# The high parts of the attentions' weights: copied by ScalarE, or brought rounded by transfers that GpSimd begins

## The chip, the cores and the metric

The kernel runs on one core of one Trainium2 chip, as one program. The metric is the device time of an execution in microseconds (us). The times before are three runs; beside them one execution was taken with the hardware profiler.

## What is computed

Three transformer layers on 256 positions of width 1024, in float32: two layers of a first kind, then one of a second kind.

```python
def hybrid_layer(x, ...):            # twice
    proj = x @ w_in
    a_in, b_in, c_in = jnp.split(proj, [A_COLS, A_COLS + B_COLS], axis=-1)
    o_a = dilated_mixture(...)        # 6 heads
    o_b = diff_attention(...)         # 4 heads
    o_c = causal_attention(...)       # 6 heads, low-rank q and kv
    h = layer_norm(DEEPNORM_ALPHA * x + heads @ w_o, ln1_g, ln1_b)
    ffn = (jax.nn.silu(h @ w_gate) * (h @ w_up)) @ w_down
    return layer_norm(DEEPNORM_ALPHA * h + ffn, ln2_g, ln2_b)

def second_block(x, c, ...):         # once
    h = _rms_norm(x, g_pre_mix[l]) * (1.0 + sc_m) + sh_m
    y = _hybrid_mixer(h, ...)         # 8 heads of sparse attention in three branches, 8 heads of indexed attention
    x = x + ga_m * _rms_norm(y, g_post_mix[l])
    h = _rms_norm(x, g_pre_ffn[l]) * (1.0 + sc_f) + sh_f
    x = x + ga_f * _rms_norm(_swiglu(h, w_gate_up[l], w_down[l]), g_post_ffn[l])
```

## The kernel before

**Three products for one.** Every large product of an activation with a weight is made of three matmuls in the type fp32r (`mm3`, lines 274 to 278). Both operands are split into a high part, the value rounded to fp32r, and a low part, the rest: high by high (L276), high by low, low by high. A low part needs its high part first. In the trace `xh`, `xl` are the parts of an activation, `hi`, `lo` those of a weight.

**Pieces of weights.** All weights come as a list of pieces, `plan`, in the order of use; a piece is 128 partitions by at most 2048 columns, 1 MB. Class `Weights` walks it. `_load` begins a piece's transfer on SP's queue into one of three `raw` buffers (L105). `_half` splits half a piece: ScalarE copies `raw` to `hi`, which rounds (L129), and VectorE subtracts `hi` from `raw` into `lo` (L130). The pools `hi` and `lo` have six half-piece buffers each, so three pieces. `get` hands out the next piece; it keeps loads three pieces ahead and splits one piece ahead. Pieces of kind "raw" are used unsplit.

**Order of the pieces.** For each of the two layers: `w_inc` (2 pieces) and `w_inbv` (in layer 1 `w_inbv` first), `w_u` raw, `w_inbqk` (2), `w_inav` (2), `w_inaqk` (3), `w_o` (4), then the feed-forward: `w_gate` and `w_up` (11 each) with `w_down` pieces among them, the last three of layer 0 and the last two of layer 1 at the end. For the second block: `w2_kc`, `w2_vc`, `w2_nq` (2 each), `w2_mi`, `w2_iq` (2), `w2_uk` raw, `w2_dq` (2), `w2_out` (4), then its feed-forward.

**Order of the work.** The program is written in order; the framework's planner gives each engine its own order from its own costs, and every engine then works its queue strictly in that order. Blocks with a raised priority are drawn forward: scores and values of the attentions, and the norms at the end of a sublayer (`ending`, L393). Matmuls of the projections fill TensorE while an attention waits for its softmax: for each pair of heads VectorE adds the bias and takes the minimum (L315), ScalarE takes the exponentials (`e`, L316), the probabilities are scaled (L550 or L552), transposed on TensorE (`pt`, L271), copied by ScalarE (`ptsb`, L586) and multiplied with the values (`ob`, L559).

**Hand-overs.** At the end of a feed-forward the last `w_down` pieces are held together while TensorE finishes rows 0 to 127 and then rows 128 to 255. The norm of the first half runs beside the matmuls of the second. Then `fill` (L861) runs the next layer's first projections on the first half, while the norm of the second half runs: `w_inbv` and `w_inc` for layer 1, `w2_kc` (`kp.run(0)`) for the second block, which later runs `kp.run(1)`, `vp.run(0)` and so on (L1129). The norms take their inverse root on GpSimd (`rsqrt`, L306 to L312), an addition and a power. GpSimd has hardly any other work.

Of the kernel before, what the change touches and what calls it, by code (L numbers as in the profile page):

```python
# [11 lines left out]
F32R = mybir.dt.float32r  # L12
AF = mybir.ActivationFunctionType
# [11 lines left out]
WARM = 11  # L25
PUTB = 2
NHI = 6
ROWS = 16
STEPS = ('00', '0001', '0001001', '0001001', '0001001')

# [61 lines left out]
class Weights:  # L92


    def __init__(self, tc, pools, plan, ahead, split_ahead):
        self.nc, self.pools, self.plan = tc.nc, pools, plan
        self.ahead, self.split_ahead = ahead, split_ahead
        self.loaded, self.split, self.at = 0, 0, 0
        self.raws, self.parts, self.out = {}, {}, {}

    def _load(self):
        i = self.loaded
# [6 lines left out]
    def start(self, pieces):  # L109
# [10 lines left out]
            self.out[i] = self._getter(i)  # L120
        self.loaded = self.split = 2

    def _half(self, i, h):
        _, _, nk, w = self.plan[i]
        t, n = self.raws[i], nk * w // 2
        hi = self.pools["hi"].tile([128, 1024], F32R, tag="hi", name="hi")
        lo = self.pools["lo"].tile([128, 1024], F32R, tag="lo", name="lo")
        c = slice(h * n, h * n + n)
        self.nc.scalar.activation(hi[:, :n], t[:, c], AF.Copy)  # L129
        self.nc.vector.tensor_tensor(lo[:, :n], t[:, c], hi[:, :n].bitcast(F32), op=OP.subtract)  # L130
        self.parts.setdefault(i, []).append((hi, lo))

# [12 lines left out]
    def _split(self):  # L145
        i = self.split
        _, kind, nk, w = self.plan[i]
        while self.loaded <= i:
            self._load()
        if kind == "split":  # L150
            for h in range(2):
                self._half(i, h)
            self.out[i] = self._getter(i)
        else:
            self.out[i] = self.raws.pop(i)
        self.split += 1

    def get(self):
        i = self.at
        self.at += 1  # L160
        n = len(self.plan)
        while self.split <= i:
            self._split()
        while self.loaded < min(n, i + 1 + self.ahead):
            self._load()
        while self.split < min(n, i + 1 + self.split_ahead) and self.plan[self.split][1] == "split":
            self._split()
        return self.out.pop(i)


@with_exitstack
def body(ctx: ExitStack, tc: tile.TileContext, io, out):
# [3 lines left out]
    def pool(name, bufs=1, **kw):  # L176
        return ctx.enter_context(tc.tile_pool(name=name, bufs=bufs, **kw))
# [4 lines left out]
    raw_p = pool("raw", 3)  # L182
    hi_p = pool("hi", NHI)
    lo_p = pool("lo", NHI)
    ln_p = pool("ln", 3)
# [22 lines left out]
    def add(name, *idx, kind="split", nk, w):  # L208
        ap = io[name]
        for i in idx:  # L210
            ap = ap[i]
        plan.append((ap, kind, nk, w))


    def add_ffn(names, idx, held):
        g, u, d = names
        for j in range(NCH):
            add(g, *idx, j, nk=8, w=256)
            add(u, *idx, j, nk=8, w=256)
            if 1 <= j <= held:  # L220
                add(d, *idx, j - 1, nk=2, w=1024)
        for j in range(held, NCH):
            add(d, *idx, j, nk=2, w=1024)

    for l in range(2):
        if l == 1:
            add("w_inbv", l, nk=8, w=256)
        for i in range(2):
            add("w_inc", l, i, nk=4, w=416)
        if l == 0:  # L230
            add("w_inbv", l, nk=8, w=256)
        add("w_u", l, kind="raw", nk=1, w=1920)
        for i in range(2):
            add("w_inbqk", l, i, nk=8, w=256)
        for i in range(2):
            add("w_inav", l, i, nk=4, w=384)
        for i in range(3):
            add("w_inaqk", l, i, nk=8, w=256)
        for i in range(4):
            add("w_o", l, i, nk=2, w=1024)  # L240
        add_ffn(("w_gate", "w_up", "w_down"), (l,), HELD[l])
    for i in range(2):
        add("w2_kc", i, nk=4, w=384)
    for i in range(2):
        add("w2_vc", i, nk=4, w=384)
    for i in range(2):
        add("w2_nq", i, nk=4, w=512)
    add("w2_mi", 0, nk=8, w=240)
    for i in range(2):
        add("w2_iq", i, nk=4, w=512)  # L250
    add("w2_uk", kind="raw", nk=1, w=896)
    for i in range(2):
        add("w2_dq", i, nk=4, w=512)
    for i in range(4):
        add("w2_out", i, nk=2, w=1024)
    add_ffn(("w2_gate", "w2_up", "w2_down"), (), HELD[2])


# [80 lines left out]
    def load_bias(oh):  # L339
# [3 lines left out]
        V.tensor_copy(bsb, pb[:10, :384])  # L343
        bd = dram.tile([ROWS, 10, 384], F32, name="bd")
        nc.scalar.dma_start(bd.rearrange("q h c -> h q c"), bsb[:, None, :].to_broadcast([10, ROWS, 384]))
        for r in range(128 // ROWS):
            p = slice(ROWS * r, ROWS * r + ROWS)
            nc.scalar.dma_start(bias[p], bass.AP(tensor=bd.tensor, offset=bd.offset + 127 - ROWS * r,
                                                 ap=[[3839, ROWS], [384, 10], [1, 256]]))

# [1019 lines left out]
```

## Time and profile before

| | |
|---|---|
| median of three runs | 979.72 us (978.67 to 981.13) |
| the profiled execution | 977.63 us, of which the span from first to last instruction 975.8 |
| TensorE matmuls, weight loads | busy 944.4 us (97%), 834.9 us (86%) |
| VectorE, ScalarE, GpSimd | busy 650.5, 533.2, 29.2 us |
| ScalarE's weight copies, L129 | 284, 293.7 us busy |
| VectorE's subtractions, L130 | 284, 339.1 us busy |
| moved by transfers | 190.55 MB |

Layer 0's attentions last until some 115 us, its feed-forward until some 320, layer 1's until some 430 and 640, the second block's attentions until some 770. In the rows, "out<-in" names the tiles written and read, "x" a count, and "<-" what ended an engine's wait. A matmul's time is its way through the array; the next begins long before it ends, so TensorE can be busy and still have gaps between starts.

### The profile page before, as it was taken

What the parts mean: (1) busy time and instruction counts of PE and PEld (TensorE: products, weight loads), DVE (VectorE), ACT (ScalarE), POOL (GpSimd) and SP (SyncE); (2) the same over time, 40 slices, a digit from 0 to 9 for tenths busy, and PEclk for the clock granted to TensorE, in tenths of its full rate; (3) what the DMA queues carried; (4) which work ended last, traced back from release to release, by engine and by line L of the source; (5) the groups of instructions that cost most, each with busy time, mean ns of one, the idle gap of its engine ahead of it and who ended that gap; (6) DMA issues with size and microseconds to landing.
All of it is one profiled execution on the core that took longest, in us unless ns stands there. A gap on an engine that the chain in (4) does not pass through costs nothing. (4 is left out here: it accounts for less than half of the span.)

```text
span 975.8 us, 16344 instructions
## 1 busy us (share of the span) xinstructions
PE 944.4 (97%) x6378; PEld 834.9 (86%) x6378; DVE 650.5 (67%) x1367; ACT 533.2 (55%) x1023; POOL 29.2 (3%) x54
## 2 busy tenths in 40 slices
PE   8999999999999999999999999889999899999997
PEld 6888689999998888878999999788666699999996
DVE  4648687767678757767767464787688665454543
ACT  4658665444444677655444444555599744344542
POOL 0000000000000100000000000101000100000000
PEclk9999999999999999999999999999999999999999
DMA  8745548877875533447875565365312156555441
GB/s 313 288 100 215 196 176 301 300 278 270 300 254 175 192 131 127 149 179 278 308 277 211 177 242 190 109 242 206 130 45 87 65 173 215 175 181 205 153 153 44
DMA packets 33456, 190.55 MB, mean 195 GB/s; under 512 B 3696, under 2 KB 5346, under 8 KB 15842
## 3 DMA queue, kind: packets, MB, share of 16 engines
q1 hardware_dynamic: 31224, 183.75, 52.9%
q10 hardware_dynamic: 2154, 5.75, 2.0%
q8 instruction: 50, 0.82, 0.3%
q14 instruction: 28, 0.23, 0.1%
HBM read 188.17 MB, written 1.32 MB: 194 GB/s over the span
## 5 line engine op out<-in xcount | busy, mean ns | idle before, releaser
L130 DVE TENSOR_TENSOR lo<-raw,hi 128x1024 fp32r<-128x1024 f32 (+3 forms) x284 | 339.1, 1202 | 99.7 <-ACT hi L129 95.6
L129 ACT ACTIVATE hi<-raw 128x1024 fp32r<-128x1024 f32 (+3 forms) x284 | 293.7, 1041 | 103.1 <-PE acc L278 52.3
L278 PE MATMUL sc<-xh,lo 128*128 128x256 f32 x960 | 271.8, 283 | 0.0
L276 PE MATMUL sc<-xh,hi 128*128 128x256 f32 x960 | 271.7, 283 | 0.0
L277 PE MATMUL sc<-xl,hi 128*128 128x256 f32 x960 | 271.7, 283 | 0.0
L276 PEld LDWEIGHTS sc<-xh,hi 128*128 128x128 f32 x960 | 184.2, 192 | 1.1
L277 PEld LDWEIGHTS sc<-xl,hi 128*128 128x128 f32 x960 | 184.2, 192 | 1.0
L278 PEld LDWEIGHTS sc<-xh,lo 128*128 128x128 f32 x960 | 184.2, 192 | 0.0
L276 PE MATMUL acc<-hi,xh 128*128 128x512 f32 (+4 forms) x384 | 135.2, 354 | 0.4 <-ACT hi L129 0.3
L277 PE MATMUL acc<-lo,xh 128*128 128x512 f32 (+4 forms) x384 | 134.0, 349 | 0.7 <-DVE lo L130 0.6
L278 PE MATMUL acc<-hi,xl 128*128 128x512 f32 (+4 forms) x384 | 133.6, 349 | 0.7 <-DVE xl L298 0.7
L276 PE MATMUL acc<-hi,hh 128*128 128x512 f32 x264 | 103.2, 391 | 0.0
L277 PE MATMUL acc<-lo,hh 128*128 128x512 f32 x264 | 103.2, 391 | 0.0
L278 PE MATMUL acc<-hi,hl 128*128 128x512 f32 x264 | 102.8, 389 | 0.0
L453 ACT ACTIVATE sg<-sc 128x256 f32<-128x256 f32 x60 | 22.6, 376 | 137.9 <-PE sc L278 137.9
L455 DVE TENSOR_TENSOR hm<-sc,sg 128x256 f32<-128x256 f32 x60 | 25.3, 421 | 88.0 <-ACT sg L453 88.0
L276 PEld LDWEIGHTS acc<-hi,xh 128*128 128x128 f32 x384 | 74.4, 194 | 8.5 <-issue 1.5
L277 PEld LDWEIGHTS acc<-lo,xh 128*128 128x128 f32 x384 | 74.4, 194 | 6.7 <-DVE lo L130 1.6
L278 PEld LDWEIGHTS acc<-hi,xl 128*128 128x128 f32 x384 | 74.2, 194 | 6.9 <-DVE xl L298 2.0
L316 ACT ACTIVATE e<-e,sm 128x128 f32<-128x128 f32 (+1 forms) x128 | 56.8, 446 | 12.0 <-DVE sm L315 7.7
L278 PEld LDWEIGHTS acc<-hi,hl 128*128 128x128 f32 x264 | 49.6, 188 | 10.8 <-DVE hl L457 0.2
L276 PEld LDWEIGHTS acc<-hi,hh 128*128 128x128 f32 x264 | 49.7, 188 | 9.8 <-ACT hh L456 0.3
(277 smaller groups left out, 1155.7 us busy)
## 6 DMA issues: line engine op xcount, KB each, us to landing
raw<-in_w_gate SPq DMA_DIRECT2D x33, 1024.0 KB, 4.9
raw<-in_w_up SPq DMA_DIRECT2D x33, 1024.0 KB, 4.9
raw<-in_w_down SPq DMA_DIRECT2D x33, 1024.0 KB, 5.0
ada<-in_w_ada SPq DMA_DIRECT2D x48, 512.0 KB, 5.2
raw<-in_w_o SPq DMA_DIRECT2D x8, 1024.0 KB, 5.2
raw<-in_w_inaqk SPq DMA_DIRECT2D x6, 1024.0 KB, 5.1
raw<-in_w_inbqk SPq DMA_DIRECT2D x4, 1024.0 KB, 6.2
gb<-in_lnrows ACTq DMA_DIRECT2D x4, 1024.0 KB, 6.2
```

What stands on the lines that cost most here:

```text
L129: self.nc.scalar.activation(hi[:, :n], t[:, c], AF.Copy)
L130: self.nc.vector.tensor_tensor(lo[:, :n], t[:, c], hi[:, :n].bitcast(F32), op=OP.subtract)
L276: T.matmul(dst, lh, rh, start=start, stop=False)
L277: T.matmul(dst, lh, rl, start=False, stop=False)
L278: T.matmul(dst, ll, rh, start=False, stop=stop)
L316: A.activation(e, e, AF.Exp, bias=nm, scale=-1.0, accum_out=sm)
L453: A.activation(sg, pg[:, 0, :], AF.Silu)
L455: V.tensor_tensor(hm, pg[:, 1, :], sg, op=OP.mult)
```

## The change

The pieces of layer 0's `w_inav`, `w_inaqk`, `w_o` and all split pieces of the attentions of layer 1 and of the second block get the kind "cast". For these, `_cast` takes two `hi` buffers and begins two transfers on GpSimd's queue, each of half a piece, from DRAM into the fp32r buffer; ScalarE's copy is left out in `_half`, and VectorE subtracts as before from the `raw` buffer, which SP's transfer still fills. `get(i)` begins these transfers for the piece i + 2, one piece before that is split. Layer 0's first pieces and all feed-forward pieces stay as they were, as do the sizes of the pools.

```diff
+SPLIT = ("split", "cast")
...
+    def _cast(self, i):
+        ap, _, nk, w = self.plan[i]
+        n = nk * w // 2
+        his = self.his[i] = []
+        for h in range(2):
+            his.append(self.pools["hi"].tile([128, 1024], F32R, tag="hi", name="hi"))
+            self.nc.gpsimd.dma_start(his[h][:, :n], ap[:, h * n:h * n + n])
...
     def _half(self, i, h):
...
-        hi = self.pools["hi"].tile([128, 1024], F32R, tag="hi", name="hi")
+        cast = i in self.his
+        hi = self.his[i][h] if cast else self.pools["hi"].tile([128, 1024], F32R, tag="hi", name="hi")
...
-        self.nc.scalar.activation(hi[:, :n], t[:, c], AF.Copy)
+        if not cast:
+            self.nc.scalar.activation(hi[:, :n], t[:, c], AF.Copy)
...
-        if kind == "split":
+        if kind in SPLIT:
+            if kind == "cast" and i not in self.his:
+                self._cast(i)
...
-        while self.split < min(n, i + 1 + self.split_ahead) and self.plan[self.split][1] == "split":
+        while self.split < min(n, i + 1 + self.split_ahead) and self.plan[self.split][1] in SPLIT:
             self._split()
+        j = self.split
+        if j < n and j == i + 1 + self.split_ahead and self.plan[j][1] == "cast":
+            self._cast(j)
...
-            add("w_inbv", l, nk=8, w=256)
+            add("w_inbv", l, kind=SPLIT[l], nk=8, w=256)
...
-            add("w_inc", l, i, nk=4, w=416)
+            add("w_inc", l, i, kind=SPLIT[l], nk=4, w=416)
...
-            add("w_inav", l, i, nk=4, w=384)
+            add("w_inav", l, i, kind="cast", nk=4, w=384)
```

`w_inbqk` becomes `SPLIT[l]` in the same way; `w_inaqk`, `w_o` and the second block's `w2_kc`, `w2_vc`, `w2_nq`, `w2_mi`, `w2_iq`, `w2_dq`, `w2_out` become "cast".

## Rows read from the trace of the kernel before

**Rows 1.** The page: TensorE's busy time; GB/s in 40 slices of 24.4 us.

```profile
PE 944.4 (97%) x6378; PEld 834.9 (86%) x6378; DVE 650.5 (67%) x1367; ACT 533.2 (55%) x1023; POOL 29.2 (3%) x54
...
GB/s 313 288 100 215 196 176 301 300 278 270 300 254 175 192 131 127 149 179 278 308 277 211 177 242 190 109 242 206 130 45 87 65 173 215 175 181 205 153 153 44
```

**Rows 2.** Groups by shape: copies and subtraction; busy us, mean ns, idle before.

```profile
L130 DVE TENSOR_TENSOR lo<-raw,hi 128x1024 fp32r<-128x1024 f32 x258 | 313.7, 1224 | 90.8 <-ACT hi L129 86.9 <-PE sc L277 1.4
...
L129 ACT ACTIVATE hi<-raw 128x1024 fp32r<-128x1024 f32 x258 | 271.7, 1058 | 97.8 <-PE acc L278 51.9 <-PE sc L277 33.6 <-PE acc L277 4.7
...
L129 ACT ACTIVATE hi<-raw 128x768 fp32r<-128x768 f32 x16 | 13.2, 840 | 3.5 <-DMA raw<-in_w_inav 1.1 <-PE sc L277 1.0 <-ACT acc L523 0.9
```

**Rows 3.** Stages: length, busy of PE, PEld, DVE, ACT, POOL, clock, DMA.

```profile
28.00:115.00 87.00, 83.94 (x581) 69.94 (x580) 58.07 (x191) 60.91 (x162) 2.40 (x3) 1.00 0.57 184
330.00:425.00 95.00, 93.13 (x644) 79.12 (x643) 62.52 (x201) 66.64 (x173) 3.26 (x5) 1.00 0.44 159
640.00:770.00 130.00, 127.56 (x802) 94.69 (x802) 99.73 (x384) 91.04 (x238) 2.62 (x6) 1.00 0.40 138
```

**Rows 4.** The same stages, busy time of the copies at L129 alone.

```profile
28.00:115.00 87.00, 21.38 (x22) 1.00 0.57 184
330.00:425.00 95.00, 23.88 (x24) 1.00 0.44 159
640.00:770.00 130.00, 27.85 (x27) 1.00 0.40 138
```

**Rows 5.** Waits of weight loads, 28 to 115 us: total, times, longest.

```profile
PEld ob L559 <- ACT ptsb L586: 1.8, 4, 0.8
PEld acc L276 <- ACT hi L129: 1.1, 2, 0.6
PEld pt L271 <- ACT ptsb L586: 1.0, 2, 0.8
```

**Rows 6.** The same, 330 to 425 us.

```profile
PEld sc L603 <- ACT e L316: 1.5, 1, 1.5
PEld ob L559 <- ACT ptsb L586: 1.2, 4, 0.4
```

**Rows 7.** The same, 640 to 770 us.

```profile
PEld ob L559 <- ACT ptsb L586: 4.5, 10, 1.0
PEld pt L271 <- ACT ptsb L586: 2.0, 4, 0.7
...
PEld pt L271 <- ACT e L316: 1.3, 4, 0.3
```

**Rows 8.** ScalarE in order of time, 309 to 327 us: start, length.

```profile
315.51 5.16 ACT L129 ACTIVATE hi<-raw 128x1024 fp32r<-128x1024 f32 x6 [0.32 <-PE acc L278]
```

**Rows 9.** ScalarE in order of time, 622 to 660 us.

```profile
626.29 0.83 ACT L129 ACTIVATE hi<-raw 128x768 fp32r<-128x768 f32 x1
...
642.46 0.85 ACT L129 ACTIVATE hi<-raw 128x768 fp32r<-128x768 f32 x1 [0.28 <-PE acc L278]
```

**Rows 10.** TensorE in order of time, 314 to 320 us.

```profile
318.85 0.28 PE L277 MATMUL acc<-lo,xh 128*128 128x256 f32 x1
```

**Rows 11.** TensorE in order of time, 640 to 648 us.

```profile
640.70 0.34 PE L277 MATMUL acc<-lo,xh 128*128 128x384 f32 x1
640.87 0.33 PE L278 MATMUL acc<-hi,xl 128*128 128x384 f32 x1
```

**Rows 12.** Transfers by kind: queue, count, KB each, median us to landing.

```profile
bias<-bd ACTq DMA_DIRECT2D x8, 160.0 KB, 10.6
...
raw<-in_w_uk SPq DMA_DIRECT2D x1, 448.0 KB, 3.5
```

**Rows 13.** GpSimd in order of time, 309 to 326 us.

```profile
311.43 0.30 POOL L311 TENSOR_SCALAR sm<-sm 128x1 f32<-128x1 f32 x1 [179.31 <-ACT acc L523]
...
323.23 0.89 POOL L311 TENSOR_SCALAR sm<-sm 128x1 f32<-128x1 f32 x1 [10.85 <-ACT acc L523]
```

More of the change, by code (lines that the diff above doesn't have):

```diff
@@ L98, in __init__ @@
         self.loaded, self.split, self.at = 0, 0, 0
-        self.raws, self.parts, self.out = {}, {}, {}
+        self.raws, self.parts, self.out, self.his = {}, {}, {}, {}
     def _load(self):
@@ L226, in body @@
         if l == 1:
-            add("w_inbv", l, nk=8, w=256)
+            add("w_inbv", l, kind=SPLIT[l], nk=8, w=256)
         for i in range(2):
-            add("w_inc", l, i, nk=4, w=416)
+            add("w_inc", l, i, kind=SPLIT[l], nk=4, w=416)
         if l == 0:
-            add("w_inbv", l, nk=8, w=256)
+            add("w_inbv", l, kind=SPLIT[l], nk=8, w=256)
         add("w_u", l, kind="raw", nk=1, w=1920)
         for i in range(2):
-            add("w_inbqk", l, i, nk=8, w=256)
+            add("w_inbqk", l, i, kind=SPLIT[l], nk=8, w=256)
         for i in range(2):
-            add("w_inav", l, i, nk=4, w=384)
+            add("w_inav", l, i, kind="cast", nk=4, w=384)
         for i in range(3):
-            add("w_inaqk", l, i, nk=8, w=256)
+            add("w_inaqk", l, i, kind="cast", nk=8, w=256)
         for i in range(4):
-            add("w_o", l, i, nk=2, w=1024)
+            add("w_o", l, i, kind="cast", nk=2, w=1024)
         add_ffn(("w_gate", "w_up", "w_down"), (l,), HELD[l])
     for i in range(2):
-        add("w2_kc", i, nk=4, w=384)
+        add("w2_kc", i, kind="cast", nk=4, w=384)
     for i in range(2):
-        add("w2_vc", i, nk=4, w=384)
+        add("w2_vc", i, kind="cast", nk=4, w=384)
     for i in range(2):
-        add("w2_nq", i, nk=4, w=512)
-    add("w2_mi", 0, nk=8, w=240)
+        add("w2_nq", i, kind="cast", nk=4, w=512)
+    add("w2_mi", 0, kind="cast", nk=8, w=240)
     for i in range(2):
-        add("w2_iq", i, nk=4, w=512)
+        add("w2_iq", i, kind="cast", nk=4, w=512)
     add("w2_uk", kind="raw", nk=1, w=896)
     for i in range(2):
-        add("w2_dq", i, nk=4, w=512)
+        add("w2_dq", i, kind="cast", nk=4, w=512)
     for i in range(4):
-        add("w2_out", i, nk=2, w=1024)
+        add("w2_out", i, kind="cast", nk=2, w=1024)
     add_ffn(("w2_gate", "w2_up", "w2_down"), (), HELD[2])
```

## Prediction

> **What bounds the kernel now.** I began with the page's busy times and its slices. TensorE is busy 97% of a span of 975.8 us [rows 1], so what an edit elsewhere can give back is what TensorE waits for that engine. The chain of waits said the same: TensorE's lines lead it. I then cut the span into stages. Transfers are to take over the copies of three of them: from the A projections of layer 0 to its output projection (28 to 115 us), layer 1's attentions (330 to 425) and the second block's (640 to 770), with the two hand-overs between a feed-forward and the next attention ahead of the last two. In these ScalarE is busy 61 of 87, 67 of 95 and 91 of 130 us [rows 3], and the copies hold 21.4, 23.9 and 27.9 us of that, a share of 0.35, 0.36 and 0.31 [rows 4] (a few of those copies are for the feed-forward behind). Last I read what the weight loads of TensorE wait for in each stage [rows 5, 6, 7]: mostly for ScalarE's copies of the transposed probabilities (ptsb) and its exponentials (e), hardly for the weight copies themselves. The reader is to see that few microseconds are there to be had.
>
> **What is removed.** 38 pieces, 76 half pieces: 9 in layer 0 (inav 2, inaqk 3, w_o 4), 14 in layer 1 (these 9, inbv 1, inc 2, inbqk 2), 15 in the second block (kc 2, vc 2, nq 2, mi 1, iq 2, dq 2, out 4). By width that is 54 halves of 1024 columns, 16 of 768 and 6 between. At 1.058 and 0.840 us [rows 2], and about 0.95 for the six, 57.1 + 13.4 + 5.7 = 76 us of ScalarE go. VectorE's subtractions stay, 1.224 us for a wide half [rows 2]; they now wait for a transfer.
>
> The gain is what TensorE waits less. Rows of ptsb and e: 1.8 + 1.0, 1.5 + 1.2, and 4.5 + 2.0 + 1.3, together 13.3 us [rows 5, 6, 7]. The share of the copies in ScalarE's time would take a third of it. A copy is among ScalarE's longest instructions, so a wait that meets one is longer than the mean; all of it would be the upper end, none the lower, since a weight load that waits may stand behind a matmul that still runs. I take 0.4, near the share: 5.3 us. The direct wait for a copy, 1.1 us in layer 0 [rows 5], I count whole, since those weights (inaqk, w_o) have long free stretches ahead of them. Ahead of the second block, a copy of 0.83 us at 626.29 stands on ScalarE between the two squares of the first norm, for whose result TensorE waits [rows 9]: 0.8 us. Together 7.2 us; bounds 0 and 13.3 + 1.1 + 0.8 = 15.2.
>
> **What is added.** 76 transfers begun by GpSimd. In bytes: 54 of 0.524 MB, 16 of 0.393 and 6 of about 0.45, 37.3 MB, on the 16 engines that move 190.55 MB now. The slices of the three stages move mostly 45 to 242 GB/s [rows 1]; the densest, 634 to 683 us, 242 and 206. The pieces there (vc1, nq, mi, iq, 6.0 MB in 43 us) add some 140, which gives 345 to 380, over the 313 that the best slice shows [rows 1]. For some 45 us that is a backlog of perhaps 10%, 4 to 5 us late at its end; the loads run ahead of their use by more than that, so I price it at nothing. If that cover were gone it would cost those 4 to 5 us.
>
> No transfer that rounds, and no transfer begun by GpSimd, is in this trace. I bound one half piece by rows. Issue: between the 0.30 and the 0.89 us of a GpSimd instruction [rows 13]; I take 0.9. Moving 0.5 MB: between the 3.5 us of a 448 KB load and the 10.6 us of the bias reads, 160 KB in short rows [rows 12]; the rows of these transfers are 3 to 4 KB like the loads', so I take 3.6. The subtraction: 1.2. So X, from a free buffer to a usable half, is 5.7 us (3.5 + 0.3 + 1.2 = 5.0 to 10.6 + 0.9 + 1.2 = 12.7), against the 1.06 + 1.2 of now.
>
> X counts only where a buffer comes free shortly before its piece is wanted. The hi pool has six halves, three pieces, so as a rule two pieces' matmuls lie between, 8 us or more. Two places are tighter. **Hand-over to layer 1:** three w_down pieces are held to the end and fill the pool. The first copy of w_inbv starts on a matmul's release at 315.51 [rows 8], and TensorE's matmul with its lo part runs at 318.85 [rows 10]: a window of 3.3 us, so 5.7 - 3.3 = 2.4 late. Behind it inc1 goes through the same queue as third piece; I allow 0.5. **Second block:** vc1 takes kc0's buffers, whose copy began at 642.46 after a wait for TensorE [rows 9]. TensorE runs these 128x384 matmuls 0.17 us apart [rows 11], and from kc0's last to vc1's first are 24, with two transposes: 4.4 us. X of a 0.39 MB half is 0.9 + 3.3 + 0.95 = 5.2: 0.8 late. Losses 2.4 + 0.5 + 0.8 = 3.7.
>
> Also moved: GpSimd, which now does little but the norms' inverse roots, gets 76 instructions that wait for buffers in the same queue. The loads on SP keep their order; each raw buffer comes free when its subtraction is done, hence as late as hi lands. And the planner orders all engines anew. I price both at nothing in the sum, and the first as a rival.
>
> **Sum.** -7.2 + 3.7 = -3.5 us. The profiled execution took 977.63 us (975.8 in the span), so 974.1; it stood 2.1 under the median of 979.72, so against the median 976.2.
>
> **Rivals.** *The gain is covered:* ScalarE's waits shrink, but TensorE fills from its other work already and only the direct terms count, 1.1 + 0.8 against 3.7 lost: +1.8, 981.5 at worst; with a part of the 5.3, about 979. For it: TensorE is busy 126 to 128 of 130 us in the last stage even by the coarse count [rows 3]. Against it: the waits for ptsb are waits of the engine that sets the end.
>
> *The rounding transfer is slow (the other side):* place, the two windows above. With X = 10 us, the middle of the upper half, they cost 6.7 + 5.6 = 12.3 - 7.2 = +5.1, 984.8. At X = 12.7 they cost 9.4 + 8.3, and nq and iq, whose windows are some 11 us (48 matmuls of 512 columns, at 0.17 x 512/384 = 0.23), about 1.5 each more: 24 - 7 = +17, 996. It decides from X = 7.5, where (X - 3.3) + (X - 4.4) is the gain. For it: nothing here shows what rounding costs a transfer. Against it: long rows.
>
> *GpSimd's queue holds an inverse root:* at 311.43 us it computes the root of layer 0's last norm [rows 13], while inbv's buffer comes free only at 315.51 [rows 8]. If the transfer stands first in the queue, the root and TensorE's transposes after it are 4.1 us late, beside which part of inbv's 2.4 is hidden: about +3.5 on the sum, 979.7 to 980.5. For it: a wait at the head of a queue stops all behind it. Against it: the norms have the higher priority, and by the planner's clock they may be ready first.
>
> *VectorE holds the descriptors back:* some VectorE instructions keep GpSimd from writing them. The bound is one VectorE instruction ahead of each late half, 1.2 us [rows 2], on the three late places: +3.6, so 979.8. The Trainium skill ("SBUF — State Buffer", Who interferes with whom) states such a lock: copies and tensor_scalar in their two-port modes shut GpSimd out, and a transfer begun by GpSimd waits for its descriptors; it speaks against this change. The same section exempts tensor_tensor, the form of the subtractions; no run so far shows either.
>
> **Chances.** Forecast 0.44 (own range 967 to 976.8: the whole 15.2 gained less 2.4 of loss, down to the bound of a visible gain). Covered 0.18. Slow transfer 0.20. Queue held 0.12, a third of it within the bound. Descriptors held 0.06. About 0.3%, 2.9 us, is what a measurement can tell here. Faster 0.44; same 0.18 + 0.06 + 0.04 = 0.28; slower 0.20 + 0.08 = 0.28. The range runs from 967 to 987: out fall the upper half of the slow transfers (0.10) and a few hundredths below.
>
> **What would show it.** A new queue with 76 transfers and 37 MB, 228 MB in all; 208 copies left at L129 and ScalarE near 457 us busy. Right: half of the ptsb and e waits gone between 700 and 770 us; TensorE waiting some 2 us for lo near 319, about 1 near 646. The size of X is read from issue to landing: under 5 us the forecast stands, over 6.5 it turns. VectorE waits for hi then name a transfer; if they are many and long among the attentions, its queue is the new brake. A root on GpSimd behind a transfer shows as TensorE waiting at 313 for the norm's result. Wrong above all if the new order of the planner moves the filler matmuls out of the attentions' gaps.

## The result and the profile after

The change made the kernel slower by 7%: 1050.78 us (median, 1048.67 to 1054.56) against 980.42 beside it, a ratio of 1.073 (interval 1.069 to 1.077), some 70 us. Forecast were 976.2 and a range up to 987. The profiled execution, the slowest of the four, has a span of 1052.8 us; it lies 77 us above that of the kernel before, the medians lie 70 apart.

The page of the changed kernel, for [rows 1]: busy times, the granted clock and GB/s in 40 slices (now of 26.3 us), and the new queue.

```profile
PE 966.1 (92%) x6378; PEld 848.0 (81%) x6378; DVE 650.3 (62%) x1367; ACT 465.5 (44%) x947; POOL 72.3 (7%) x130
...
PEclk9988999999999999989999999999989999999999
...
GB/s 320 329 289 91 200 178 289 292 275 266 299 251 195 309 234 142 229 249 200 309 271 221 200 222 195 204 273 277 265 98 161 120 81 201 200 161 200 167 155 40
...
q0 software_dynamic: 10944, 37.29, 11.3%
```

The edit does what it says: 76 instructions fewer on ScalarE, 37.3 MB on a new queue, and ScalarE at 465.5 us where I had expected 457. The reader is to see that TensorE's share fell from 97% to 92%. Its work is the same 6378 matmuls, so it waits more; its busy time rose as well, by 21.7 us.

The stages for [rows 3], moved to where they now lie, with the same columns (the last three: clock, DMA share, GB/s).

```profile
28.00:140.00 112.00, 89.54 (x582) 73.78 (x581) 59.30 (x193) 45.40 (x144) 12.58 (x21) 0.91 0.70 222
355.00:475.00 120.00, 105.19 (x672) 89.08 (x671) 62.38 (x205) 48.33 (x155) 16.45 (x28) 0.94 0.66 224
690.00:845.00 155.00, 136.32 (x802) 98.72 (x803) 99.57 (x384) 67.81 (x212) 15.18 (x30) 0.94 0.57 192
```

All three attention stages are some 25 us longer; VectorE's and ScalarE's work in them fits easily, and the granted clock, 1.00 before, is 0.91 and 0.94 on average. In the second block the same 802 matmuls were busy 136.3 us instead of 127.6 [rows 3]. To place the loss I measured every kernel between the same events, GpSimd's powers for the first half of each norm (that of layer 0's first norm begins at 121.98 us before and at 147.11 after, and so on). Before, layer 0 up to that norm takes 122.0 us, layer 1's attentions 119.6, the second block's 147.1; after, 25.1, 24.6 and 24.7 us more. The feed-forwards stay within 1 us; 2.7 more come after the last root. Together these are the 77 us of the profiled executions.

Next, what VectorE waited for in the changed kernel (total, times, longest).

```profile
DVE lo L141 <- DMA hi<-in_w_o: 24.6, 8, 5.5
DVE lo L141 <- DMA hi<-in_w_inaqk: 21.6, 8, 10.9
...
DVE lo L141 <- DMA hi<-in_w_dq: 9.5, 2, 5.1
DVE lo L141 <- DMA hi<-in_w_nq: 8.4, 2, 8.2
```

With those of inav, inbv, inbqk, kc, vc, iq and out these are 88 us. Not all of that is new: in the same three stages of the kernel before, VectorE's subtractions waited 28 us for ScalarE's copies. ScalarE's wait for VectorE's half of the softmax grew too; here the row of before and under it that of after.

```profile
ACT e L316 <- DVE sm L315: 7.7, 10, 1.9
```

```profile
ACT e L332 <- DVE sm L331: 43.2, 19, 12.1
```

How one such wait reaches TensorE is seen in layer 0 of the changed kernel, in order of time: VectorE, ScalarE's queue, TensorE's weight loads (start, length; idle time before, and what ended it).

```profile
60.22 1.23 DVE L141 TENSOR_TENSOR lo<-raw,hi 128x1024 fp32r<-128x1024 f32 x1 [0.67 <-DMA hi<-in_w_inaqk]
72.37 1.23 DVE L141 TENSOR_TENSOR lo<-raw,hi 128x1024 fp32r<-128x1024 f32 x1 [10.93 <-DMA hi<-in_w_inaqk]
74.25 1.23 DVE L141 TENSOR_TENSOR lo<-raw,hi 128x1024 fp32r<-128x1024 f32 x1 [0.66 <-DMA hi<-in_w_o]
77.57 1.22 DVE L141 TENSOR_TENSOR lo<-raw,hi 128x1024 fp32r<-128x1024 f32 x1 [2.09 <-DMA hi<-in_w_o]
78.71 0.28 DVE L331 CUSTOM_DVE_ANT_0 e<-sc,cst 128x128 f32<-128x128 f32 x1
...
58.00 14.85 ACTq L364 DMA_DIRECT2D bias<-bd  x7
...
79.72 0.50 PEld L287 LDWEIGHTS pt<-cst,e 128*128 128x128 f32 x3 [13.27 <-issue]
```

The windows of 10 us there, columns as in [rows 3]:

```profile
70.00:80.00 10.00, 0.24 (x2) 0.26 (x3) 4.88 (x12) 2.44 (x11) 0.00 (x0) 0.50 1.16 276
80.00:90.00 10.00, 10.00 (x60) 8.04 (x61) 5.94 (x33) 9.07 (x34) 0.00 (x0) 0.72 0.27 107
```

From 60 to 78.7 us VectorE does four subtractions and nothing else, because each waits for its transfer and the softmax stands behind them in its queue. ScalarE's queue stands over the bias reads at the same time. TensorE waits 13.3 us for probabilities to transpose; "issue" there means that no single releaser shows. The granted clock is 0.50, the lower of its two levels (1.2 GHz), in the ten microseconds in which TensorE did next to nothing, and 0.72 on average in the next ten.

The transfers of the changed kernel, for [rows 12]: queue, count, KB, median us to landing.

```profile
raw<-in_w_gate SPq DMA_DIRECT2D x33, 1024.0 KB, 5.0
raw<-in_w_o SPq DMA_DIRECT2D x8, 1024.0 KB, 8.0
hi<-in_w_o POOLq DMA_DIRECT2D x16, 512.0 KB, 6.6
hi<-in_w_inaqk POOLq DMA_DIRECT2D x12, 512.0 KB, 5.6
...
bias<-bd ACTq DMA_DIRECT2D x8, 160.0 KB, 12.8
...
hi<-in_w_mi POOLq DMA_DIRECT2D x2, 480.0 KB, 9.0
```

The rounding transfers land after 5.6 to 9 us in all groups but two (out and kc, 3.9 and 3.7), not after 3.6. The loads of w_o, 8.0 us, are late too; those of the feed-forwards, with no rounding transfer beside them, are not.

### The profile page after: what moved, and what is told of

It reads as the page before. It is cut to its first block, busy times and chain, and to the rows that moved or that the text cites. A ratio compares the mean times of both kernels' runs of the same rounds, so it can differ in the third digit from the quotient of the medians.

```text
span 1052.8 us, 16425 instructions
## 1 busy us (share of the span) xinstructions
PE 966.1 (92%) x6378; PEld 848.0 (81%) x6378; DVE 650.3 (62%) x1367; ACT 465.5 (44%) x947; POOL 72.3 (7%) x130
## 3 DMA queue, kind: packets, MB, share of 16 engines
q0 software_dynamic: 10944, 37.29, 11.3%
## 4 chain that ended last, share of the span: by engine, by line
PE 40%; issue 4%; DMA 3%; DVE 3%; ACT 2%; POOL 1%; POOLq 0%; DVEq 0%; ACTq 0%
PE sc L294 7%; PE sc L293 7%; PE sc L292 7%; PE acc L293 5%; PE acc L292 5%; PE acc L294 5%; DVE lo L141 1%; PE pt L287 1%; DMA hi<-in_w_nq 1%; DMA hi<-in_w_iq 1%; DMA hi<-in_w_dq 1%; PE sc L628 1%; DMA hi<-in_w_kc 0%; PE sc L619 0%; POOL hi L130 0%
## 5 line engine op out<-in xcount | busy, mean ns | idle before, releaser
L140 ACT ACTIVATE hi<-raw 128x1024 fp32r<-128x1024 f32 (+1 forms) x208 | 219.0, 1057 | 89.0 <-PE acc L294 48.3
L292 PE MATMUL acc<-hi,xh 128*128 128x512 f32 (+4 forms) x384 | 138.3, 362 | 6.2 <-DMA hi<-in_w_nq 2.8
L293 PE MATMUL acc<-lo,xh 128*128 128x512 f32 (+4 forms) x384 | 136.8, 357 | 4.3 <-DVE lo L141 4.2
L294 PE MATMUL acc<-hi,xl 128*128 128x512 f32 (+4 forms) x384 | 136.9, 359 | 0.3 <-DVE xl L314 0.3
```

Of the source, the lines that this page charges most:

```text
L292: T.matmul(dst, lh, rh, start=start, stop=False)
L293: T.matmul(dst, lh, rl, start=False, stop=False)
L294: T.matmul(dst, ll, rh, start=False, stop=stop)
```

## The experiments

Lengths are against the profiled execution of before, in the stages named above: layer 0 up to its first norm, layer 1's attentions, the second block's. They come from one profiled execution of each kernel. Medians are over all executions of a kernel; the kernel before took 978.3 to 980.4 beside them. The profiled execution without high parts took 1000.3, some 6 us over its median, so its three columns add up to more than the median lost.

| kernel | median us | layer 0 | layer 1 | second block |
|---|---|---|---|---|
| changed | 1050.78 | +25.1 | +24.6 | +24.7 |
| no high parts | 993.95 | +14.7 | +3.9 | +6.4 |
| low parts on GpSimd | 1099.75 | +22.6 | +45.6 | +49.8 |
| low parts written late | 1049.44 | +28.0 | +21.4 | +21.9 |
| 8 hi, 2 raw buffers | 1047.09 | +27.7 | +9.2 | +22.6 |
| before, extra traffic | 990.29 | +2.0 | +6.2 | +3.8 |
| changed, bias by SP | 1047.72 | +24.5 | +22.2 | +20.7 |
| no high parts, bias by SP | 1000.69 | +14.5 | +5.4 | +6.3 |
| low parts without high parts | 1017.64 | +13.1 | +16.0 | +9.0 |
| copies by GpSimd | 1014.00 | +11.3 | +11.7 | +10.4 |
| no high parts, ordered | 991.51 | +4.8 | +5.3 | +6.3 |
| before, ordered (control) | 981.96 | +2.8 | +0.2 | +1.6 |
| short copies, ordered | 988.26 | +4.8 | +4.7 | +2.8 |

**Without high parts.** In `_cast` nothing is taken or begun, and in `_half`:

```diff
+        if cast:
+            hi, o = lo, (1 - h) * n
+            self.nc.vector.tensor_tensor(lo[:, :n], t[:, c], t[:, o:o + n], op=OP.subtract)
```

> This kernel leaves out the high parts of the 38 cast pieces: neither a copy nor a transfer makes them, the matmuls read the low part twice, and the low part is a subtraction within the raw buffer, of the same shape and length; its values are not the reference's. It is the change with a transfer that costs nothing and is never late. Theory A (ScalarE's relief is worth what the prediction's first step said, the loss is all in the transfers): 7.2 us faster than before, so about 973, at best 965, and ScalarE's weight copies at 208. Rival B (the relief is covered, TensorE fills these gaps anyway): 978 to 981. Rival C (the loss is not the transfers but the planner's other order of the engines, which any edit of these copies brings): slower than before by a good part of the 70 us, over 1000.

It took 993.95, ratio 1.016 (1.013 to 1.019). Neither A nor B: with transfers that cost nothing the kernel is still slower. C holds in kind, but it is 15 of the 70 us. The trace shows one place of this loss. VectorE's subtractions of these pieces have no high part to wait for, and now stand in its queue for a `lo` buffer that TensorE's matmuls free; before, all its subtractions together waited 1.4 us for TensorE.

```profile
DVE lo L142 <- PE acc L297: 17.1, 16, 4.2
```

ScalarE's exponentials waited 21.2 us for VectorE, against 7.7 before.

**VectorE's queue and the transfers' lead.** Three kernels, each an edit of the changed one.

```diff
+        eng = self.nc.gpsimd if cast else self.nc.vector
+        eng.tensor_tensor(lo[:, :n], t[:, c], hi[:, :n].bitcast(F32), op=OP.subtract)
```

```diff
-        while self.split < min(n, i + 1 + self.split_ahead) and self.plan[self.split][1] in SPLIT:
+        while self.split < min(n, i + 1 + self.split_ahead) and self.plan[self.split][1] == "split":
...
+        for j in range(i + 1, min(n, i + 2 + self.split_ahead)):
+            if j not in self.his and self.plan[j][1] == "cast":
+                self._cast(j)
```

```diff
+    raw_p = pool("raw", 2)
+    hi_p = pool("hi", 8)
```

> The changed kernel, but the 76 subtractions that wait for a rounding transfer are on GpSimd, so VectorE's queue holds nothing that waits for one. Theory Q (VectorE works strictly in order and stands at these subtractions, some 88 us in all, while the softmax behind them is ready): VectorE's waits for these transfers are gone, the waits of the exponentials for VectorE (43 us after the change, 7.7 before) fall under 15, and the time falls to 985 to 1010. Rival T (the high parts simply come too late for TensorE, or the transfers crowd each other out, whichever engine subtracts): 1035 or more, and TensorE's waits name the transfers or GpSimd's low parts. A subtraction on GpSimd is not in any trace so far; if it took over 3 us a half, GpSimd's queue would be late itself and Q would show only in VectorE's waits.

> The changed kernel, but the subtraction of a cast piece is written where the piece is handed out, one piece later than now, while its transfers begin where they began. Theory Q (VectorE's queue is held by subtractions that stand too early in it): the planner may place them later, VectorE's waits for transfers fall from some 88 to under 45 us and the time to 1000 to 1030. Rival T (late for TensorE whichever way): no faster than 1045, more likely slower, since each piece's first low part, 1.2 us, is now in front of its matmuls: up to 38 x 1.2 = 46 us more.

> The changed kernel with eight hi half-buffers instead of six, paid for with two raw buffers instead of three (loads run two pieces ahead). A rounding transfer then finds its buffer free one piece earlier. Theory W (the transfer is late because its buffer comes free late; its own 6 to 9 us would be hidden if it began a piece earlier): GpSimd's wait for buffers and VectorE's for transfers fall by more than half, the three attention stages lose under 10 us each instead of 25, time 990 to 1015, plus what the missing raw buffer costs in the feed-forwards (0 to 10, seen in their stages). Rival T2 (the transfer engines are crowded, and a transfer that begins earlier lands no earlier against its use): 1035 or more.

The first was no clean test. GpSimd's subtraction, in this group of its trace, took 2.39 us and it stood waiting for transfers in the queue that also begins the next ones; the brake had only moved, and the time rose by 49 us.

```profile
L142 POOL TENSOR_TENSOR lo<-raw,hi 128x1024 fp32r<-128x1024 f32 x54 | 128.6, 2388 | 139.1 <-DMA hi<-in_w_o 41.8 <-DMA hi<-in_w_out 29.7 <-DMA hi<-in_w_inaqk 29.6
```

The second changed little: VectorE's waits for the transfers stayed at 92 us, presumably since the planner places a subtraction where by its own clock the transfer has landed, wherever it is written. The third took most of the loss out of layer 1 (24.6 to 9.2) and none out of the second block. Over the whole of that kernel VectorE's waits for hi fell from 88 to 14 us, and 42 us of waits for raw came instead, as with two raw buffers the loads were late. W holds for layer 1; for the rest the test is spoiled by its price.

**Traffic alone.** The copies of before stay, and beside them:

```diff
+            j = self.pools["dram"].tile([128, 1024], F32R, tag="junk", name="junk", bufs=4)
+            d = self.nc.gpsimd.dma_start(j[:, :n], ap[:, h * n:h * n + n])
```

> The kernel before, ScalarE's copies and all, and beside it the same 76 rounding transfers begun by GpSimd, each released by the copy of the piece ahead, into a scratch buffer in DRAM that nobody reads. So the traffic is the changed kernel's and nothing waits for it. Theory T2 (the transfer engines are crowded: loads and reads of the bias come late because 37 MB more go the same way): a good part of the 70 us, over 1010, with raw loads landing at 6.5 us and more in the attentions. Theory L (traffic alone is harmless; the loss comes from a rounding transfer standing between a free buffer and the subtraction): under 992, at most the bias reads of layer 0 are hit.

> Nothing of the reference is computed; the kernel times transfers of 0.5 MB (128 rows of 4 KB) by themselves: one after the other, plain begun by SP, plain begun by GpSimd, rounding begun by GpSimd; then six at once of each kind; then two rounding ones beside four plain ones; then rounding ones one after the other while VectorE copies without a break, and while it subtracts. Theory R (rounding or GpSimd's way of beginning makes a transfer slow): a rounding one alone takes 6 us or more where a plain one of SP takes under 4. Theory T2 (crowding): alone all kinds take 3 to 4.5 us and six at once 8 or more for the last. Rival V (VectorE holds GpSimd's descriptors back): beside VectorE's copies a rounding transfer takes longer by 1 us or more, beside subtractions not.

The extra traffic costs 10.5 us, ratio 1.011 (1.009 to 1.012): L, with a part of T2. The kernel of transfers alone consists of stretches such as this one, with a barrier between:

```python
for _ in range(4):
    t = p.tile([128, 1024], F32R, tag="rone", name="rone", bufs=1)
    nc.gpsimd.dma_start(t, src[i])
    A.activation(z[:, 0, 0:1], t[:, 0:1], AF.Copy, scale=0.0)
```

By itself a rounding transfer is as fast as a plain one; transfers by kind (queue, count, KB, median us to landing).

```profile
spsix<-in_w SPq DMA_DIRECT2D x6, 512.0 KB, 5.8
...
rsix<-in_w POOLq DMA_DIRECT2D x6, 512.0 KB, 6.5
spone<-in_w SPq DMA_DIRECT2D x4, 512.0 KB, 3.3
gpone<-in_w POOLq DMA_DIRECT2D x4, 512.0 KB, 3.6
rone<-in_w POOLq DMA_DIRECT2D x4, 512.0 KB, 3.5
...
rmix<-in_w POOLq DMA_DIRECT2D x2, 512.0 KB, 7.0
```

"one" is one after the other, "six" six at once, "rmix" two beside four plain ones. The time to landing runs from the start of the issue: a rounding transfer begun at 33.27 us was read at 36.85. Rounding and GpSimd add 0.2 to 0.7 us; company nearly doubles the time. R falls, and crowding alone makes 3.5 into 6.5 and 7.0, near the 5.6 to 9 of the kernel. Beside VectorE's copies GpSimd's beginning of a transfer took 0.63, 0.74 and 0.92 us instead of 0.53 (a plain one with nothing beside it took 0.66 once), beside its subtractions 0.53; the slowest landed after 4.1 us:

```profile
104.03 0.92 POOL L49 DMA_DIRECT2D rcopy<-in_w  x1 [3.44 <-ACT z L26]
...
113.16 0.53 POOL L49 DMA_DIRECT2D rsub<-in_w  x1 [8.21 <-SPq L86]
```

**The bias reads.** In the changed kernel and in that without high parts:

```diff
-            nc.scalar.dma_start(bias[p], bass.AP(tensor=bd.tensor, offset=bd.offset + 127 - ROWS * r,
+            nc.sync.dma_start(bias[p], bass.AP(tensor=bd.tensor, offset=bd.offset + 127 - ROWS * r,
```

> The changed kernel, with the attentions' bias, written and read back once in layer 0, begun by SP instead of ScalarE, which puts its reads ahead of the loads of w_o. Theory B (in layer 0 ScalarE stands in its queue at the bias reads, 14.4 us against 3.6 before the change, because the loads of w_o and the rounding transfers now run at the same time): ScalarE's wait falls under 5 us, layer 0's attentions lose under 17 us instead of 25, time 1036 to 1044. Rival Q (VectorE standing at the subtractions of inaqk and w_o sets layer 0 anyway): no faster than 1047.

> The kernel without high parts for the cast pieces (the matmuls read the low part twice, values are not the reference's) and with the bias begun by SP. It was 15 us slower than before with the bias on ScalarE. Theory B: nearly all of that was the collision of bias reads and w_o loads, so 976 to 983. If ScalarE's relief is worth anything, under 975. Rival C (the planner's other order costs it): 988 or more.

B falls both times: ScalarE's stand at the bias reads is gone, layer 0 takes as long, and the second kernel is not faster but 6.7 us slower by its median, though the ranges of the two overlap. The second trace shows what else goes on there. First before, then the kernel without high parts and with the bias by SP: VectorE in order of time, copies of the A projections (`qkA`; ScalarE makes the other three) and the first softmax of the B heads (`e<-sc,bias`); the last row of the second is a weight load of TensorE.

```profile
66.66 0.42 DVE L825 COPY qkA<-acc 128x256 f32<-128x256 f32 x1
70.54 0.29 DVE L315 CUSTOM_DVE_ANT_0 e<-sc,bias 128x128 f32<-128x128 f32 x1
...
83.91 0.42 DVE L825 COPY qkA<-acc 128x256 f32<-128x256 f32 x1
...
93.13 0.42 DVE L825 COPY qkA<-acc 128x256 f32<-128x256 f32 x1
```

```profile
72.49 0.42 DVE L844 COPY qkA<-acc 128x256 f32<-128x256 f32 x1 [4.52 <-PE acc L297]
78.25 0.42 DVE L844 COPY qkA<-acc 128x256 f32<-128x256 f32 x1 [5.33 <-PE acc L297]
84.00 0.42 DVE L844 COPY qkA<-acc 128x256 f32<-128x256 f32 x1 [5.33 <-PE acc L297]
84.35 0.29 DVE L334 CUSTOM_DVE_ANT_0 e<-sc,bias 128x128 f32<-128x128 f32 x1
...
111.92 0.51 PEld L622 LDWEIGHTS sc<-qkA 64*128 64x128 f32 x4 [8.12 <-DVE sm L334]
```

Before, the projections are spread among the softmaxes of the B heads, until 93 us. Without high parts they run in one piece ahead of them, and when the attentions come TensorE has nothing to fill with: it stands 8.1 us.

**Only TensorE waits.** The transfers are real and TensorE reads them; the low part is made as in the kernel without high parts.

> The changed kernel with its 76 rounding transfers, which TensorE reads, but the low part of a cast piece is a subtraction of the two halves of the raw buffer, of the same shape, which does not wait for the transfer; its values are not the reference's. Only TensorE itself can now wait for a rounding transfer. Theory Q (VectorE, strictly in order, stands at the subtractions for some 88 us in all and holds up the softmax): the time falls to what the kernel without high parts takes (994) plus the price of the traffic (10), so 995 to 1015. Rival T (the high parts are late for TensorE whichever way): 1035 or more, with TensorE's waits naming the transfers.

1017.64: of the 70 us, 33 go when VectorE no longer waits for a transfer. Q is right, if 3 us above its bound. Over order and traffic (994 + 10.5) 13 us are left, and TensorE's own waits for the transfers are of that size (in the changed kernel they are 4.6 us); its weight loads in this kernel:

```profile
PEld acc L296 <- DMA hi<-in_w_inc: 5.1, 3, 2.6
...
PEld acc L296 <- DMA hi<-in_w_nq: 4.6, 3, 2.2
...
PEld acc L296 <- DMA hi<-in_w_vc: 2.0, 2, 1.4
```

The softmax is not free in this kernel either: ScalarE's exponentials wait 33.1 us for VectorE, whose subtractions stand 19.5 us for `lo` buffers. So the 33 us are what the waits for transfers cost, and not all that VectorE's queue costs.

**ScalarE relieved otherwise, and the order restored.** GpSimd copies, with no transfer; and, in the kernel without high parts and with the bias by SP, the first matmul of each A projection, of both layers, is tied to a score matmul:

```diff
+        if cast:
+            self.nc.gpsimd.tensor_copy(hi[:, :n], t[:, c])
```

```diff
+                        if k == 0:
+                            at = score_mm[-5 + min(2 * j + f, 4)]
+                            tc.add_manual_dep(m.ins, at.ins.name,
+                                              mybir.DependencyInfo(mybir.DependencyClass.Sync, mybir.DependencyReason.DATA),
+                                              reason="order")
```

> ScalarE is relieved of the same 76 copies in another way: GpSimd copies raw to the high part, no transfers are added. No copy of GpSimd's is in a trace so far; its subtraction of a wide half took 2.24 us. If ScalarE's relief were worth the 7.2 us of the prediction's first step and only the transfers spoiled it: 970 to 978. Theory C (the relief is worth nothing, and another order of the planner costs some 15 us as without high parts): 985 to 1005. If GpSimd's copy is over 3 us, or slows VectorE beside it: over 1005.

> The kernel without high parts and with the bias begun by SP (1000.7), in which TensorE did all six A projections of layer 0 in one run, from 69 to 84 us, ahead of the B heads' softmax, and stood 8 us later with none left. Here dependencies between TensorE's own instructions put each A projection of both layers behind the score matmuls beside which it ran before the change (the first behind the last C pair, the second to fourth behind the first three B pairs, the last two behind the fourth). Nothing else is changed. Theory C (the planner's order moved the filler matmuls out of the attentions' gaps): layer 0's attentions, 14 us too long, come back to under 5 too long, and the time to 980 to 990. Rival: the order is not it, 996 or more. If ScalarE's relief is worth anything it shows as a time under 978.

> The kernel before with ScalarE's copies, and with the two edits of the last kernel without high parts: the bias begun by SP and the A projections tied behind the same score matmuls. It is that kernel's control: the two differ by ScalarE's 76 copies alone. If it takes 978 to 982, as the kernel before does, the ties and the bias cost nothing, and the 991.5 of the kernel without the copies means that relieving ScalarE gains nothing even when it is free, and that some 11 us of the planner's other order remain in the stages without ties. If it takes 988 or more, the ties themselves cost what remained, and ScalarE's relief is worth about nothing. If it is faster than 976, the order was not the best before, and this is the version to keep.

GpSimd's copy took 1.31 us for a wide half, but the kernel took 1014, without any transfer. VectorE waited 35.7 us for these copies, and its own busy time rose from 650.5 to 674.6 us for the same 1367 instructions (its subtractions took up to 2.06 us, before at most 1.23): GpSimd's copies slow what VectorE does beside them, as the expectation feared. How much of the 34 us is either, or the order, the run does not separate. The ties brought layer 0 from +14.5 to +4.8 and the time from 1000.7 to 991.5, and on the kernel before they cost next to nothing (ratio 1.0017, 1.0007 to 1.0028). So the order of these projections was the main cause in layer 0, and with it restored the freed ScalarE still gains nothing. In layer 1 the same ties changed nothing (+5.4 and +5.3). The last kernel keeps the copies, in place and waited for (the subtraction `b` is tied to the copy `a`), 2 columns wide.

```diff
+            short = self.pools["hi"].tile([128, 1024], F32R, tag="hi", name="hi")
+            a = self.nc.scalar.activation(short[:, :2], t[:, h * n:h * n + 2], AF.Copy)
```

> The kernel without high parts, bias on SP, A projections tied (991.5; its control with full copies 982.0), but ScalarE's 76 copies are back in their places with their buffers, and the subtraction waits for them as before; each is 2 columns wide instead of 768 to 1024, some 0.2 us instead of 1.06. The matmuls read the low part twice, values are not the reference's. It removes the duration of the copies and nothing else: if ScalarE's time was worth what the prediction's first step said, 7 us under the control, 973 to 977. If the relief is worth nothing and the planner's order costs the rest: 982 to 993, and TensorE's waits for the transposed probabilities are what they are with full copies.

988.26, ratio 1.009 (1.008 to 1.011). TensorE's waits for the transposed probabilities and the exponentials, first in the control, then with short copies:

```profile
PEld ob L560 <- ACT ptsb L587: 8.1, 20, 1.1
...
PEld pt L271 <- ACT ptsb L587: 3.1, 8, 0.7
PEld pt L271 <- ACT e L317: 1.7, 5, 0.3
PEld sc L605 <- ACT e L317: 1.5, 1, 1.5
```

```profile
PEld ob L584 <- ACT ptsb L611: 7.1, 18, 0.9
...
PEld pt L295 <- ACT ptsb L611: 3.3, 11, 0.5
...
PEld ob L584 <- ACT e L575: 0.4, 1, 0.4
```

ScalarE is busy 474.3 us instead of 533.8 in the control, and of the 11.2 us for ptsb 0.8 are gone. These waits are the length of the chain from transposing to copying, not a queue behind weight copies. The waits for exponentials, with the rows not shown, fell from 3.9 to 1.0 us, 1.5 of it a single wait; whether the shorter copies did that or the other order, these runs do not show, and the kernel's time has no gain of it.

## Why the prediction was wrong

The sign was wrong, and by far. Step by step:

- *The gain, 7.2 us.* At most some 3, and none of it in the time: the waits for ptsb hardly move when the copies shrink to 0.2 us, and those for e fall by 2.9. The rows themselves were read rightly [rows 5 to 7]; the cause of the ptsb waits was not. "A copy is among ScalarE's longest instructions, so a wait that meets one is longer than the mean" was the reason for taking 0.4; the short copies show that few waits for ptsb met one.
- *X, from a free buffer to a usable half.* Alone it is shorter than the 5.7 us taken: 3.5 + 1.2 = 4.7, since the time to landing holds the issue, 0.53 us, which the sum added once more as 0.9. In the kernel it is 6.6 + 1.2 = 7.8 us for w_o, just over the 7.5 from which the slow transfer was to decide; through crowding, not rounding.
- *Where X counts.* This is the step that failed most: "X counts only where a buffer comes free shortly before its piece is wanted". I asked when TensorE wants the piece. But the subtraction stands in VectorE's queue long before, ahead of a softmax, and a late transfer stops that at once. The two places I priced behaved much as said. At the hand-over to layer 1 the weight loads waited 2.06 and 1.01 us for inbv's parts, X being 6.0 us (begun at 340.91, the low part read at 346.87), against 2.4 + 0.5 forecast; at vc they waited 1.4 us for the transfer and 0.9 for the low part, against 0.8. The other halves, priced at nothing, cost most of the 33 us of VectorE's queue. The sentence that VectorE's "queue is the new brake" if its waits were many stood among the signs, without a price.
- *"The planner orders all engines anew", priced at nothing.* 15 us without any transfer, 21 with the bias by SP. Tying the A projections gave 9 of the 21 back, all in layer 0, where these fillers had left the attentions' gaps. What made it wrong "above all" by my own last sentence is the second cause.
- *The backlog, 4 to 5 us if its cover were gone.* 10.5 with traffic alone by the medians. In the profiled execution 3.8 us are added in the second block, for which I had priced it, 8.2 in the two layers, where I expected none, and 2.7 behind the last root. The cover was not there: beside the extra transfers the loads of w_o land after 8.8 us, before after 5.2.
- *GpSimd's queue holding an inverse root.* Not where I priced it: at the hand-over, on GpSimd in order of time, the root came first. It did happen later in layer 1, where three transfers stood between the two instructions of a root and the power began 2.99 us after the addition (360.30 and 363.29), 0.32 us before the change; no run shows what that cost.

```profile
336.93 0.56 POOL L328 TENSOR_TENSOR sm<-sm,mhalf 128x1 f32<-128x1 f32 x1
340.91 1.23 POOL L130 DMA_DIRECT2D hi<-in_w_inbv  x2 [3.42 <-PE acc L294]
```

- *VectorE holding the descriptors.* The issue took at most 0.4 us longer beside copies, and no longer beside subtractions. The rule of the Trainium skill ("SBUF — State Buffer", Who interferes with whom), that copies in a two-port mode keep GpSimd from writing descriptors and tensor_tensor does not, agrees with these rows; here it is too small to matter.

The pieces add up roughly: 15 (order, no transfers) + 10.5 (traffic) + 33 (VectorE's queue) = 58.5 of 70. The waits of TensorE itself, 5.1 + 4.6 + 2.0 = 11.7 us in the kernel where it alone waits, come near the rest; in the changed kernel itself those are 4.6 us. Each kernel has its own order, so this is a sum of differences and no strict division. The lower granted clock is inside these costs and not a further one: in the place shown it fell while TensorE stood.

Open stays why 6 us remain over the control with short copies, mostly in layer 1 (4.7 against 0.2). Its A projections were tied too, without effect. There VectorE's subtractions stand 12.8 us for `lo` buffers, none in the control, and the exponentials wait 11.3 us for VectorE, 4.5 in the control. Another order of the planner with the same brake is the likely cause; it is argued, not shown. No version beat the kernel before: with ScalarE's copies free or 0.2 us short, the best took 988.

## What to carry to other kernels

A value that an in-order engine turns into another one is wanted when that engine's queue reaches it, not when its last reader does; so price a late transfer at the engine that waits for it and at what is queued behind. Before trusting a relief, look whether the waits in question are queueing behind the work to be removed, or only the length of their own chain. And where a planner orders the engines, an edit that removes work is also a new order: a control that ties the part of the order in question shows how much of what was measured is order.

## What the runs showed that was not expected

- A rounding transfer begun by GpSimd is hardly slower alone than a plain one of SP (3.5 against 3.3 us for 0.5 MB), and six at once follow each other by 1.2 to 2.3 us, plain ones of SP by 1.2 to 1.6.
- GpSimd copies 128x1024 from float32 to fp32r in 1.31 us, near ScalarE's 1.06; its subtraction of that size takes 2.39, twice VectorE's. With those 76 copies on GpSimd, VectorE was busy 24 us longer for the same instructions.
- The issues of seven bias reads held ScalarE's queue for 14.85 us when the loads of w_o and rounding transfers ran beside them, and for 13.93 us without high parts, so without any rounding transfer. Before, eight issues took 4.02, with the extra traffic 4.31.
- Each of the seven whole kernels with transfers begun by GpSimd ends 2.7 us later behind its last root, also where nobody reads what they bring; the others end as before, within 0.1 us.
